# A hybrid decoder layer on one core: another order of the pieces in the gate and up units, and a regrouped last step

## The chip, the cores and the metric

The kernel runs on one core of one Trainium2 chip. The metric is the device time of one execution in microseconds (us), as the median of several runs. Engines: TensorE (matmul, PE in the rows; its weight loads are PEld), VectorE (DVE), ScalarE (ACT), GpSimd (POOL) and SyncE (SP, which issues most of the loads). A row's L73 is line 73 of the kernel.

## The reference

One layer over 256 tokens of width 2048, in float32, with a hidden width of 5632:

```python
h = h + 0.5 * swiglu(rmsnorm(h, ffn1_norm), ffn1_w_gu, ffn1_w_down)
proj = rmsnorm(h, mix_norm) @ w_in
...                     # spatial gating, Mamba-2 scan, output projection, cross attention
h = h + 0.5 * swiglu(rmsnorm(h, ffn2_norm), ffn2_w_gu, ffn2_w_down)
return rmsnorm(h, final_norm)

def swiglu(x, w_gu, w_down):
    g, u = jnp.split(x @ w_gu, 2, axis=-1)
    return (jax.nn.silu(g) * u) @ w_down
```

The change touches the two feed-forward layers (`swiglu`), the making of operands from transposes, and the final norm.

## The kernel before

Every float32 product is made of three float32r products: each operand is split into a high half (a cast on ScalarE, `high`, line 161) and a low half (what is left, a subtraction on VectorE, `split_op`, line 169), and high x high, high x low and low x high are added up. The weights come from memory in pieces of 256 rows by 2 x 512 columns (`load`, on SP's queue, three raw buffers), are split on the way (three buffers for high halves, two for low ones) and are used once.

A feed-forward layer runs in units. A gate and up unit c (0 to 10) computes 512 gate columns and 512 up columns for both token tiles of 128, from eight pieces of the contraction. `proj_sum` takes a piece in one of two ways. A C piece ("ordinary") is 24 matmuls of 512 columns into the four banks m2, m3, m4 and c11, one after another. An S piece forms the product in the manner of Strassen: `split_sums` makes four sums of weight blocks on VectorE, and seven products (21 matmuls) go into the banks m2, m3, m4 and four more, m1, m6, m5 and m7, which only S pieces use. An S piece so spares TensorE three matmuls and costs VectorE more. Its first products (m1, m2, m3) need the plain blocks, the later ones the sums. When the last S piece of a unit has its four own banks done, `mid` adds them up into four parts (line 503; m1 is copied by ScalarE, line 470), and in the last piece of the unit `evac` adds each of the four other banks to a part as it is finished, applies SiLU (ScalarE, line 527) and multiplies gate and up (line 530).

`GU_KINDS = "CSCSCSCC"` gives the kind of each piece of the contraction; `order` the order in which they are taken. Unit c = 0 has kinds and an order of its own (`FIRST_KINDS`, `FIRST`): six C pieces, an S piece, a C piece. All other units take theirs in the order of the string. After units 0 to 4, and after units 5 to 10, `add_sum` multiplies the hidden chunks with the down weights, in two halves with pieces of both kinds (`DN_KINDS`, C C S at the start).

The hidden chunk of a unit (512 columns, two pieces of the next product's operand) is put off by one step with `later`: after the first piece of the following unit, TensorE transposes its two halves into two banks of the same eight that the products use (tag "bank"), four transposes each. A half is then emptied by `to_operand` (for a C piece: high half on ScalarE, line 346, low half on VectorE, line 347) or by `Pieces.sums` (for an S piece: a copy on ScalarE, line 417, then from SBUF three differences and two splits, lines 424 to 430). With a norm's weights as a scale (`c0` given), `to_operand` works on the two columns of its bank by themselves, lines 352 and 353. Nothing else is put off into the units c > 0; jobs that fall between the first and the last S piece wait until it is over.

The matmuls keep their order in the program; the order on the other engines is fixed when the kernel is built, by a planner that goes by readiness and program order, except where `behind` puts an instruction behind another on its engine.

At the end, `finish(n, t, added)` runs for each quarter n of the width and token tile t, behind the last addition to it (`added`): squares on ScalarE with a running sum, the multiplication by the norm's weights, and for n = 3 the reciprocal root (two small VectorE steps, a power on GpSimd) and the scaling of all four quarters with their output transfers (256 KB each, on SP's, ScalarE's or GpSimd's queue). The two scalings of token tile 0 on VectorE are held until the last addition to token tile 1 (`scale_first`).

Of the kernel before, what the change touches and what calls it, by code (L numbers as in the profile page):

```python
# [8 lines left out]
F32 = mybir.dt.float32  # L9
F32R = mybir.dt.float32r  # L10
AF = mybir.ActivationFunctionType
ALU = mybir.AluOpType
AX = mybir.AxisListType
# [3 lines left out]
P = 128  # L17
D = 2048
S = 256
NT = S // P  # L20
DFF = 5632
# [9 lines left out]
EPS = 1e-6  # L31
BIG = 3.0e38
NC = 512
# [13 lines left out]
def hybrid_layer(ctx: ExitStack, tc: tile.TileContext, x, mem, w_gu1, w_dn1, w_in, w_s, w_out,  # L47
                 w_q, w_kv, w_o, w_gu2, w_dn2, cols, rows, gm_vn, fin, out):
    nc = tc.nc
# [11 lines left out]
    small = ctx.enter_context(tc.tile_pool(name="small", bufs=2))  # L61
# [37 lines left out]
    h = [const.tile([P, NT, NC], F32, name=f"h{n}") for n in range(4)]  # L99
# [7 lines left out]
    col = const.tile([P, N_COLS], F32, name="col")  # L107
# [44 lines left out]
    def behind(instructions):  # L152

        order = ExitStack()
        for ins in instructions:
            order.enter_context(tc.issue_after(ins))
        return order
# [87 lines left out]
    def proj_sum(w, r0, xps, kinds, cs, mid, evac, order=None, fine=0):  # L245
        n = len(kinds)
        order = list(range(n)) if order is None else order
        s_at = [m for m, i in enumerate(order) if kinds[i] == "S"]
        c_at = [m for m, i in enumerate(order) if kinds[i] == "C"]
        banks = {}  # L250

        def product(name, pairs, stop):
            start = name not in banks
            if start:
                banks[name] = side("acc")
            seq = [x for ah, al, bh, bl in pairs for x in ((ah, bh), (ah, bl), (al, bh))]
            for m, (a, b) in enumerate(seq):
                matmul(banks[name], a, b, start=start and m == 0, stop=stop and m == len(seq) - 1)

        for m, i in enumerate(order):  # L260
            end = m == n - 1
            key = (id(w), r0, i, cs)
            sums = kinds[i] == "S"
            raw = ready.pop(key) if key in ready else load(w, r0 + i * KP * P, cs, FOR_SUMS if sums else PLAIN)
            if sums:
                parts = split_sums(raw)
                x = xps[i]
                names = ["m1", "m2", "m3", "m6", "m5", "m7", "m4"]
                if m == s_at[-1]:
                    names = ["m1", "m6", "m5", "m7", "m2", "m3", "m4"]  # L270
                for name in names:
                    f, b = {**SOWN, **SHARED}[name]
                    product(name, [(x[:, 0, f], x[:, 1, f], *parts[b])],
                            m == s_at[-1] if name in SHARED else end)
                    if m == s_at[-1] and name == "m7":
                        mid([banks[k] for k in ("m1", "m6", "m5", "m7")])
            else:
                x = xps[i]
                with behind(xps.made[i] if m < fine else ()):
                    hi, lo = split(raw, m < fine)  # L280

                turns = [((t, j), range(KP)) for t, j in HOME]
                if m < fine:
                    turns = [((t, j), (k,)) for k in range(KP) for j in range(2) for t in range(NT)]
                for a, ((t, j), ks) in enumerate(turns):
                    name = HOME[t, j]
                    product(name, [(*tokens(x, k, t), hi[:, 2 * k + j], lo[:, 2 * k + j]) for k in ks],
                            m == (c_at[-1] if name == "c11" else n - 1))
                    if end and ks[-1] == KP - 1:
                        evac(t, j, banks[name])  # L290
                    if a == len(turns) // 2 - 1:
                        step(shut=s_at[0] <= m < s_at[-1], of=0.5)
                step(shut=s_at[0] - 1 < m < s_at[-1], of=0.5)
                continue
            step(shut=s_at[0] - 1 < m < s_at[-1])
# [27 lines left out]

    def sum_sq(ss, src):
        junk = half_k(F32, "junk")
        nc.scalar.activation(junk, src, AF.Square, accum_out=ss)

    def rstd_of(ss, name):
        n = ss.shape[1]
# [8 lines left out]
    def to_operand(srcs, dst, q, c0=None, of=None):  # L338
        of = q if of is None else of
        ps = side("tpose").rearrange("p (k s) -> p k s", k=2)  # L340
        for k in range(2):
            for t in range(NT):
                transpose(out=ps[:, k, t * P:(t + 1) * P],
                          in_=srcs[t][:, (of + k) * P:(of + k + 1) * P], identity=ident)
        if c0 is None:
            hi = nc.scalar.copy(out=dst[:, q:q + 2, :S], in_=ps)
            lo = nc.vector.tensor_tensor(out=dst[:, q:q + 2, S:], in0=ps,  # L347
                                         in1=dst[:, q:q + 2, :S].bitcast(F32), op=ALU.subtract)
        else:
            for k in range(2):  # L350
                sc = col[:, c0 + of + k:c0 + of + k + 1]
                hi = nc.scalar.activation(dst[:, q + k, :S], ps[:, k, :], AF.Copy, scale=sc)
                lo = nc.vector.scalar_tensor_tensor(out=dst[:, q + k, S:], in0=ps[:, k, :], scalar=sc,
                                                    in1=dst[:, q + k, :S].bitcast(F32),
                                                    op0=ALU.mult, op1=ALU.subtract)
        return hi.ins, lo.ins
# [146 lines left out]
        nc.vector.tensor_tensor(out=out, in0=a, in1=b, op=op)  # L503


    GU_KINDS = "CSCSCSCC"

    FIRST_KINDS, FIRST = "CCCCCSCC", [0, 2, 4, 6, 1, 3, 5, 7]

# [2 lines left out]
    def ffn(nrm, w_gu, w_dn, done=None, each=None, fine=0):  # L512
        for c_from, c_to in ((0, 5), (5, 11)):
            kinds, turn = DN_KINDS[c_to - c_from]
            hts = Pieces(kinds, "hid", nrm.xts)
            for c in range(c_from, c_to):
                m = {}
                gs = []

                def mid(banks):  # L520
                    m["m1"], m["y"], m["z"], m["y2"] = parts_of(banks)

                def evac(t, j, ps):
                    g, u = (m["z"], m["y2"]) if t else (m["m1"], m["y"])
                    if j == 0:
                        total(g, ps, g, ALU.subtract if t else ALU.add)
                        nc.scalar.activation(g, g, AF.Silu, scale=nrm.rstd[:, t:t + 1])
                        return
                    total(u, ps, u)
                    nc.vector.scalar_tensor_tensor(out=g, in0=u, scalar=nrm.rstd[:, t:t + 1], in1=g,  # L530
                                                   op0=ALU.mult, op1=ALU.mult)
                    gs.append(g)

                if c == 0:
                    proj_sum(w_gu, 0, nrm.xts, FIRST_KINDS, (c * NC, DFF + c * NC), mid, evac, FIRST, fine)
                else:
                    proj_sum(w_gu, 0, nrm.xts, GU_KINDS, (c * NC, DFF + c * NC), mid, evac)
                hts.later(gs)
            last = c_to == 11
            add_sum(w_dn, c_from * NC, hts, (kinds, kinds), turn, 0.5, done if last else None, each if last else None)  # L540
# [480 lines left out]

    fws = {}

    scale_first = []

    def finish(n, t, added):
        if n not in fws:
            fws[n] = half_k(F32, "fw")
            nc.gpsimd.dma_start(out=fws[n], in_=fin[:, n * NC:(n + 1) * NC].broadcast_to([P, NC]))
        sum_sq(ss_f[:, t, n:n + 1], h[n][:, t, :])  # L1030
        if n < 2 or t == 0:
            nc.vector.tensor_tensor(out=h[n][:, t, :], in0=h[n][:, t, :], in1=fws[n], op=ALU.mult)
        if n < 3:
            return
        if t:

            with behind([added.ins]):
                scale_first.pop()()
        r = rstd_of(ss_f[:, t:t + 1, :], f"f{t}")

        def scale(m):
            o = h[m][:, t, :]
            if m < 2:
                nc.scalar.mul(o, o, r)
            elif t:
                nc.vector.scalar_tensor_tensor(out=o, in0=o, scalar=r, in1=fws[m], op0=ALU.mult, op1=ALU.mult)
            else:
                nc.vector.tensor_scalar(out=o, in0=o, scalar1=r, scalar2=None, op0=ALU.mult)
            queue = nc.sync if m > 1 else nc.scalar if t else nc.gpsimd
            queue.dma_start(out=o_v[:, t, m * NC:(m + 1) * NC], in_=o)  # L1050

        for m in (0, 1):
            if t:
                scale(3 - m)
            scale(m)
        if not t:
            scale_first.append(lambda: (scale(3), scale(2)))

    ffn(n2, w_gu2, w_dn2, each=finish)
    assert not put_off  # L1060
# [31 lines left out]
```

## Time and profile before

| | |
|---|---|
| median of 3 runs | 2500.37 us (2499.86 to 2500.73) |
| the profiled execution | 2500.98 us |
| its span, first to last instruction | 2499.2 us |
| TensorE busy / weight loads busy | 2467.2 us / 2104.5 us |
| VectorE busy | 1967.4 us |
| ScalarE busy | 1291.7 us |
| granted TensorE clock | 0.999 |

The span lies inside the profiled time; the terms of a sum are read from the span's rows and set against that execution's own time. Busy times are shares of the whole span; what a wait costs is read from the stretch in which it stands.

### The profile page before, as it was taken

To read this page: it belongs to the slowest core of one execution; us is meant where nothing else is said; L and a number is where in the kernel's file an instruction comes from. 1 tells how busy PE (TensorE), PEld (TensorE's weight loads), DVE (VectorE), ACT (ScalarE), POOL (GpSimd) and SP (SyncE) were. 2 spreads that over 40 slices of the span, in tenths; PEclk is the share of its full clock that TensorE was granted. 3 is DMA by queue.
4 is the path that set the end of the run, shared out by engine and by line. 5 is a ranking of instruction groups with operands and counts; after the bars stand their busy time and mean duration, and the time that the engine had idled before them with its cause. 6 is when DMAs were issued, how large, how long until landed. Compare 5 with 4: busy or idle time off the path is not lost.

```text
span 2499.2 us, 31437 instructions
## 1 busy us (share of the span) xinstructions
PE 2467.2 (99%) x12673; PEld 2104.5 (84%) x12673; DVE 1967.4 (79%) x1832; ACT 1291.7 (52%) x1164; POOL 20.6 (1%) x46
## 2 busy tenths in 40 slices
PE   9999999999999999999999999999999999999998
PEld 7888887888889998888888999988887888878886
DVE  7988889888877677655698755678899888898887
ACT  6555445555546454435555544455555545455554
POOL 0000000000000000000000000000000000000000
PEclk9999999999999999999999999999999999999999
DMA  7655665565654555545566655555555666656664
GB/s 239 194 195 188 205 207 191 188 196 190 202 178 165 194 182 201 203 152 187 186 199 202 219 170 168 169 180 174 191 195 189 200 198 199 194 185 206 197 203 151
DMA packets 205762, 476.75 MB, mean 191 GB/s; under 512 B 15040, under 2 KB 17248, under 8 KB 204848
## 3 DMA queue, kind: packets, MB, share of 16 engines
q1 hardware_dynamic: 202800, 464.31, 57.0%
q0 software_dynamic: 1840, 9.26, 1.0%
q8 instruction: 99, 1.62, 0.3%
q10 hardware_dynamic: 976, 1.18, 0.1%
q14 instruction: 47, 0.39, 0.0%
HBM read 472.57 MB, written 2.13 MB: 190 GB/s over the span
## 4 chain that ended last, share of the span: by engine, by line
PE 81%; DVE 9%; issue 7%; ACT 2%; DMA 1%; SPq 0%; DVEq 0%; POOL 0%; POOLq 0%; ACTq 0%
PE acc L73 77%; DVE lo L169 3%; ACT hi L161 2%; DVE part L503 2%; DVE sum L169 1%; PE tpose L76 1%; DVE part L530 1%; PE yp L73 1%; PE logits L73 0%; PE o L73 0%; DVE hid L347 0%; DVE cacc L622 0%; DMA raw<-in_w_dn 0%; DMA raw<-in_w_gu 0%; PE mixed L73 0%
## 5 line engine op out<-in xcount | busy, mean ns | idle before, releaser
L161 ACT CAST hi<-raw 128x2048 fp32r<-128x2048 f32 (+1 forms) x438 | 791.3, 1807 | 865.0 <-PE acc L73 726.9
L169 DVE TENSOR_TENSOR lo<-raw,hi 128x2048 fp32r<-128x2048 f32 (+2 forms) x446 | 949.3, 2130 | 327.5 <-PE acc L73 223.3
L73 PE MATMUL acc<-hi,xp_ffn 128*128 128x512 f32 x1824 | 576.0, 390 | 0.4 <-ACT hi L183 0.4
L73 PEld LDWEIGHTS acc<-hi,xp_ffn 128*128 128x128 f32 x1824 | 342.4, 188 | 72.1 <-ACT hi L183 1.1
L73 PE MATMUL acc<-lo,xp_ffn 128*128 128x512 f32 x912 | 355.2, 389 | 0.4 <-DVE lo L169 0.4
L169 DVE TENSOR_TENSOR lo<-sum,hi 128x2048 fp32r<-128x2048 f32 x109 | 249.8, 2292 | 45.3 <-ACT hi L161 45.3
L73 PE MATMUL acc<-hi,hid 128*128 128x512 f32 x896 | 282.6, 390 | 0.0
L161 ACT CAST hi<-sum 128x2048 fp32r<-128x2048 f32 x109 | 208.8, 1915 | 93.2 <-DVE sum L169 75.9
L73 PE MATMUL acc<-hi,xt_mix 128*128 128x512 f32 x768 | 241.7, 393 | 0.0
L73 PEld LDWEIGHTS acc<-lo,xp_ffn 128*128 128x128 f32 x912 | 171.3, 188 | 36.7 <-DVE lo L169 1.4
L73 PEld LDWEIGHTS acc<-hi,hid 128*128 128x128 f32 x896 | 168.2, 188 | 34.7
L73 PE MATMUL acc<-xt_mix,hi 128*128 128x256 f32 x1024 | 186.0, 284 | 0.0
L73 PE MATMUL acc<-lo,hid 128*128 128x512 f32 x448 | 174.5, 390 | 0.0
L503 DVE TENSOR_TENSOR part<-acc,part 128x512 f32<-128x512 f32 x240 | 160.8, 686 | 14.0 <-ACT part L470 7.3
L73 PEld LDWEIGHTS acc<-hi,xt_mix 128*128 128x128 f32 x768 | 144.2, 188 | 30.3 <-issue 0.5
L73 PEld LDWEIGHTS acc<-xt_mix,hi 128*128 128x128 f32 x1024 | 159.6, 192 | 0.3
L73 PE MATMUL acc<-hi,xp_ffn1s 128*128 128x512 f32 x466 | 151.6, 393 | 8.0 <-DVE hid L347 8.0
L73 PE MATMUL acc<-hi,xp_ffn2s 128*128 128x512 f32 x466 | 151.6, 393 | 8.0 <-DVE hid L347 8.0
L169 DVE TENSOR_TENSOR sum<-sum,raw 128x512 f32<-128x512 f32 x218 | 150.4, 690 | 5.2
L73 PE MATMUL acc<-lo,xt_mix 128*128 128x512 f32 x384 | 149.7, 390 | 0.0
L73 PE MATMUL acc<-xt_mix,lo 128*128 128x256 f32 x512 | 145.2, 284 | 0.7 <-DVE lo L169 0.7
L169 DVE TENSOR_TENSOR sum<-raw 128x1024 f32<-128x1024 f32 x109 | 132.7, 1217 | 0.0
(280 smaller groups left out, 3377.8 us busy)
## 6 DMA issues: line engine op xcount, KB each, us to landing
raw<-in_w_gu SPq DMA_DIRECT2D x286, 512.0 KB, 3.9
raw<-in_w_in SPq DMA_DIRECT2D x80, 1024.0 KB, 5.1
raw<-in_w_dn SPq DMA_DIRECT2D x60, 1024.0 KB, 5.4
raw<-in_w_gu SPq DMA_DIRECT2D x132, 256.0 KB, 4.1
raw<-in_w_kv SPq DMA_DIRECT2D x28, 1024.0 KB, 5.3
raw<-in_w_out SPq DMA_DIRECT2D x21, 1024.0 KB, 5.6
raw<-in_w_q SPq DMA_DIRECT2D x16, 1024.0 KB, 5.1
raw<-in_w_dn SPq DMA_DIRECT2D x28, 512.0 KB, 4.0
```

The source lines that it names most:

```text
L73: return pe(nc.tensor.matmul(out, lhsT=lhsT, rhs=rhs, start=start, stop=stop))
L76: return pe(nc.tensor.transpose(out=out, in_=in_, identity=identity))
L161: nc.scalar.copy(out=t[:, :n], in_=x[:, :n])
L169: last_split[:] = [nc.vector.tensor_tensor(**kw).ins]
L503: nc.vector.tensor_tensor(out=out, in0=a, in1=b, op=op)
L530: nc.vector.scalar_tensor_tensor(out=g, in0=u, scalar=nrm.rstd[:, t:t + 1], in1=g, op0=ALU.mult, op1=ALU.mult)
```

## The change

The units c > 0 take their pieces in the order 0, 2, 1, 4, 3, 6, 5, 7, which makes their kinds C C S C S C S C. In `to_operand` with a scale, both high halves are issued before both low halves. In `finish`, the sum over the first three quarters of the squares is made ahead (`pre`), so that one small step is left behind the last squares; all four scalings of token tile 0, on ScalarE too, now stand behind the last addition and the last squares of token tile 1; and each token tile is scaled in the order 3, 0, 2, 1.

```diff
     def sum_sq(ss, src):
         junk = half_k(F32, "junk")
-        nc.scalar.activation(junk, src, AF.Square, accum_out=ss)
+        return nc.scalar.activation(junk, src, AF.Square, accum_out=ss)
...
+            scs = [col[:, c0 + of + k:c0 + of + k + 1] for k in range(2)]
             for k in range(2):
-                sc = col[:, c0 + of + k:c0 + of + k + 1]
-                hi = nc.scalar.activation(dst[:, q + k, :S], ps[:, k, :], AF.Copy, scale=sc)
-                lo = nc.vector.scalar_tensor_tensor(out=dst[:, q + k, S:], in0=ps[:, k, :], scalar=sc,
+                hi = nc.scalar.activation(dst[:, q + k, :S], ps[:, k, :], AF.Copy, scale=scs[k])
+            for k in range(2):
+                lo = nc.vector.scalar_tensor_tensor(out=dst[:, q + k, S:], in0=ps[:, k, :], scalar=scs[k],
...
-    GU_KINDS = "CSCSCSCC"
+    GU_KINDS, GU_ORDER = "CSCSCSCC", [0, 2, 1, 4, 3, 6, 5, 7]
...
-                    proj_sum(w_gu, 0, nrm.xts, GU_KINDS, (c * NC, DFF + c * NC), mid, evac)
+                    proj_sum(w_gu, 0, nrm.xts, GU_KINDS, (c * NC, DFF + c * NC), mid, evac, GU_ORDER)
...
-        sum_sq(ss_f[:, t, n:n + 1], h[n][:, t, :])
+        squares = sum_sq(ss_f[:, t, n:n + 1], h[n][:, t, :])
...
+        if n == 2:
+
+            pre[t] = small.tile([P, 1], F32, name=f"pre{t}", bufs=1)
+            nc.vector.tensor_reduce(out=pre[t], in_=ss_f[:, t:t + 1, :3], axis=AX.X, op=ALU.add)
+            nc.vector.tensor_scalar(out=pre[t], in0=pre[t], scalar1=1.0 / D, scalar2=EPS, op0=ALU.mult, op1=ALU.add)
         if n < 3:
             return
         if t:
 
-            with behind([added.ins]):
+            with behind([added.ins, squares.ins]):
                 scale_first.pop()()
-        r = rstd_of(ss_f[:, t:t + 1, :], f"f{t}")
+        r = small.tile([P, 1], F32, name=f"rstd_f{t}", bufs=1)
+        ms = small.tile([P, 1], F32, name="ms")
+        nc.vector.tensor_scalar(out=ms, in0=ss_f[:, t, 3:4], scalar1=1.0 / D, scalar2=pre[t], op0=ALU.mult, op1=ALU.add)
+        nc.gpsimd.tensor_tensor(out=r, in0=ms, in1=neghalf[:, :1], op=ALU.pow)
...
-        for m in (0, 1):
-            if t:
-                scale(3 - m)
-            scale(m)
-        if not t:
-            scale_first.append(lambda: (scale(3), scale(2)))
+        def scale_all():
+            for m in (3, 0, 2, 1):
+                scale(m)
+
+        if t:
+            scale_all()
+        else:
+            scale_first.append(scale_all)
```

## Rows read from the trace of the kernel before

**Rows 1.** The page's busy times: us, share of the span, instructions.

```profile
PE 2467.2 (99%) x12673; PEld 2104.5 (84%) x12673; DVE 1967.4 (79%) x1832; ACT 1291.7 (52%) x1164; POOL 20.6 (1%) x46
```

**Rows 2.** TensorE's waits, whole span: waiter, awaited, us, times, longest.

```profile
PE acc L73 <- DVE hid L347: 16.1, 16, 1.3
PE acc L73 <- DVE lo L169: 3.4, 9, 0.8
```

**Rows 3.** Busy times of stretches from transpose to transpose: stretch, length, each engine.

```profile
63.95:106.40 42.45, 42.45 (x193) 35.10 (x192) 38.31 (x33) 22.58 (x16) 0.00 (x0) 1.00 0.61 198
106.40:238.36 131.96, 128.00 (x574) 105.29 (x573) 117.54 (x108) 69.00 (x53) 0.00 (x0) 1.00 0.60 195
385.46:602.91 217.45, 213.38 (x956) 175.50 (x955) 192.20 (x168) 113.28 (x83) 0.00 (x0) 1.00 0.61 196
1871.03:2002.99 131.96, 128.00 (x574) 105.32 (x573) 117.63 (x108) 68.90 (x53) 0.00 (x0) 1.00 0.60 195
2150.09:2367.57 217.48, 213.39 (x956) 175.50 (x955) 192.34 (x168) 113.22 (x83) 0.00 (x0) 1.00 0.60 195
```

**Rows 4.** Timeline, unit c = 2: start, us, engine, line, tiles [idle before].

```profile
107.19 0.48 PE L73 MATMUL acc<-hi,xp_ffn1s 128*128 128x512 f32 x1
...
108.09 2.28 DVE L169 TENSOR_TENSOR lo<-raw,hi 128x2048 fp32r<-128x2048 f32 x1
...
111.43 0.68 DVE L347 TENSOR_TENSOR hid<-tpose,hid 128x512 fp32r<-128x512 f32 x1
...
112.17 0.50 PE L73 MATMUL acc<-hi,xp_ffn1s 128*128 128x512 f32 x1 [1.32 <-DVE hid L347]
```

**Rows 5.** Timeline around the end of unit c = 0, and of c = 1.

```profile
52.54 2.28 DVE L169 TENSOR_TENSOR lo<-raw,hi 128x2048 fp32r<-128x2048 f32 x1
...
53.06 0.39 PE L73 MATMUL acc<-hi,xp_ffn 128*128 128x512 f32 x1
...
63.79 2.28 DVE L169 TENSOR_TENSOR lo<-sum,hi 128x2048 fp32r<-128x2048 f32 x1
...
64.74 0.48 PE L73 MATMUL acc<-hi,xp_ffn1s 128*128 128x512 f32 x1
...
85.67 2.28 DVE L169 TENSOR_TENSOR lo<-raw,hi 128x2048 fp32r<-128x2048 f32 x1
```

**Rows 6.** VectorE's groups by shape, 107 to 284 us, those of the hidden chunks.

```profile
L429 DVE TENSOR_TENSOR hids<-forms,hids 128x512 fp32r<-128x512 f32 x6 | 4.1, 684 | 0.0
L347 DVE TENSOR_TENSOR hid<-tpose,hid 128x512 fp32r<-128x512 f32 x5 | 3.3, 685 | 0.5 <-ACT hid L346 0.5
...
L424 DVE TENSOR_TENSOR forms<-forms 128x256 f32<-128x256 f32 x3 | 1.3, 418 | 0.0
```

**Rows 7.** Timeline at the start of the first down projection, which takes C C S.

```profile
241.03 1.29 DVE L347 TENSOR_TENSOR hid<-tpose,hid 128x512 fp32r<-128x512 f32 x2 [0.46 <-ACT hid L346]
243.32 2.29 DVE L169 TENSOR_TENSOR lo<-sum,hi 128x2048 fp32r<-128x2048 f32 x1 [1.00 <-ACT hi L161]
...
244.69 0.39 PE L73 MATMUL acc<-hi,hids 128*128 128x512 f32 x1
```

**Rows 8.** Timeline at the kernel's start.

```profile
7.42 0.47 ACT L352 ACTIVATE xp_ffn<-tpose,col 128x256 fp32r<-128x256 f32 x1 [0.55 <-DVE xp_ffn L353]
...
9.18 0.50 PE L73 MATMUL acc<-lo,xp_ffn 128*128 128x512 f32 x1 [0.22 <-DVE lo L169]
```

**Rows 9.** Timeline of the end; the transfers' rate in 40 slices, 2485 to 2500 us.

```profile
2489.45 0.69 DVE L464 SCALAR_TENSOR_TENSOR h<-acc,h 128x512 f32<-128x512 f32 x1
...
2490.20 1.33 ACT L1044 ACTIVATE h<-h,rstd_f 128x512 f32<-128x512 f32 x2 [0.66 <-POOL rstd_f L334]
...
2491.44 0.61 ACT L326 ACTIVATE junk<-h 128x512 f32<-128x512 f32 x1
...
2492.61 0.58 POOL L334 TENSOR_TENSOR rstd_f<-ms,neghalf 128x1 f32<-128x1 f32 x1 [0.23 <-DVE ms L333]
...
GB/s 0 0 0 0 0 0 0 0 0 0 0 0 0 0 0 0 0 180 371 361 360 366 404 361 350 55 289 388 393 361 388 393 366 230 0 0 0 0 0 0
```

More of the change, by code (lines that the diff above doesn't have):

```diff
@@ L1022, in hybrid_layer @@
     fws = {}
-    scale_first = []
+    scale_first, pre = [], {}
     def finish(n, t, added):
```

## The prediction

> **What bounds the kernel now.** I began with the busy times by engine [rows 1]. TensorE is busy 2467.2 of the 2499.2 us, so 32 us of the span are without a matmul, and a change that issues the same matmuls, as this one does, can only win from those 32 us and from what a stopped TensorE needs to come up to pace again. Next came the list of TensorE's waits [rows 2]: 16 waits of about 1 us, 16.1 us in all, are for line 347, the VectorE half of `to_operand` that empties a transpose bank of a hidden chunk. 3.4 us more are waits for a weight's low half, nine of them; the rest is single waits at the start and the time before the first and after the last matmul.
>
> The third view, the busy times of stretches [rows 3], gives the true price of those waits. I cut it at the transposes that each gate and up unit issues after its first piece, so a stretch is a whole number of units. The stretch without a wait takes 42.45 us and TensorE is busy in all of it: that is the floor of a unit. Three units take 131.96, five take 217.45 and 217.48. So the waits cost 131.96 - 3 x 42.45 = 4.61 and 217.45 - 5 x 42.45 = 5.20 us in the first feed-forward layer, 4.61 and 5.23 in the second, 19.65 us together: 16.1 idle, 3.5 in slower first matmuls behind the stops.
>
> The timeline of one such unit shows the mechanism [rows 4]. The first S piece begins at 107.19, right behind the transposes. It opens its last four banks one after another; of the eight, four are held by the C piece before it and two by the transposes. VectorE does the low half of a C piece first (108.09, 2.28 us) and reaches the hidden chunk's bank at 111.43. The matmul that wants this bank starts at 112.17, after 1.32 us of idleness. What is late is VectorE's turn, not its strength: it is busy 38.31 of the 42.45 us.
>
> **The new piece order.** No matmul, split or load is added or dropped. The units go C C S C S C S C instead of C S C S C S C C. Read across the boundary both are three C pieces and then S C S C S, so loads on SP's queue, raw buffers and splits follow one another as now; only the boundary moves one C piece back. The transposes still come after the unit's first piece, but then a second C piece follows, which opens no bank, and only then the S piece. A C piece lasts (63.95 - 53.06)/2 = 5.45 us, the left edge of the first stretch being where the transposes stand [rows 3, 5]. So VectorE has 5.45 us more before anyone wants the bank, against a wait of 1.32. I take all 19.65 us as won; the bounds are 0 and 19.65.
>
> What this needs is that VectorE isn't late elsewhere, since the four parts and the four evacuations now follow the last S piece with one C piece left in the unit, not two. The trace of before has this boundary once, because the unit c = 0 already ends in S C [rows 5]. With its last C piece beginning at 53.06 and the next S piece at 64.74 (11.68 later), VectorE had done parts, evacuations and the S piece's splits by 63.79 + 2.28 = 66.07, 13.0 after the last S piece; they are first needed after nine matmuls of 5.45/24 = 0.227 us, at 11.68 + 2.04 = 13.7, and no wait stands there. In the new order the S piece begins a C piece later, and its last low half is due at 13.7 + 5.45 = 19.2. VectorE has in addition a C piece's low half (2.29) and the hidden chunk: at most three sums of 0.42 and three low halves of 0.69, 3.3 us [rows 6]. 13.0 + 2.29 + 3.3 = 18.6, which is 0.6 us in time even from that start. An ordinary unit starts better: there the low half of the piece after the last S piece begins at 85.67, 4.4 before that S piece ends (106.40 - 3 x 5.45 = 90.05), while at the boundary of c = 0 it began at 52.54, 0.5 before. So the margin is about 0.6 at the worst boundary and 0.6 + 3.9 = 4.5 us at the others.
>
> The second likeness is the down projection, which already begins C C S with the same transposes after its first piece [rows 7]. There VectorE emptied both banks from 241.03, began the S piece's last low half at 243.32, and the S piece began at 244.69 without a wait, its last low half (done 245.6) 1.1 us ahead of need.
>
> The Trainium skill speaks against the order: "Perfetto Trace Analysis", section Matmul Optimizations, wants all eight PSUM banks in use. With two C pieces in front, four accumulating banks serve alone for 5.45 us longer; by that rule the unit would gain nothing and the time stay near 2500, by the down projection's rows it loses nothing by it.
>
> **High halves together.** In `to_operand` with a scale the second high half waited 0.55 us for VectorE's first low half [rows 8]; now it follows the first high half, and VectorE's work comes after both. During matmuls this is hidden. At the very start TensorE waits for it: the second kind of product began at 9.18 after waiting for a low half. The gain there is between 0 and 0.55 us; some of it comes back as longer waits for low halves later in c = 0, where such waits of up to 0.8 us stand already [rows 2]. I take 0.1.
>
> On the order itself the Trainium skill ("PSUM — Partial Sum Buffer", section on bank collisions) says that two engines may not be in one bank at a time, even reading; the 0.55 us wait agrees, and by it the gain needs both ScalarE passes ahead of VectorE, as in the diff. It leaves the sum as it is.
>
> **The tail.** The last addition ends at 2489.45 + 0.69 = 2490.14. Its squares start at 2491.44, because ScalarE scales token tile 0 first (1.33 us from 2490.20); rstd is there at 2493.19 [rows 9]. In the new order the squares start at 2490.20, 1.24 sooner. On VectorE the two small pre-sums and token tile 0's two scalings stand ahead of the rest, so I take rstd 1.1 sooner. ScalarE then scales four pieces behind the squares, from about 2490.95 to 2493.6, where it ended near 2493.19 + 1.33 = 2494.5. Of the outputs, eight transfers of 256 KB, the rate row shows traffic from about 2491.4 to 2497.6 with one hole near 2494.4; 2.1 MB at about 375 GB/s need 5.6 us, so they can't end before 2497.0. The value is -0.6. If GpSimd issues token tile 0's two output transfers ahead of the second rstd (it waits for ScalarE's scalings until 2492.3 and then issues), rstd comes near 2493.7 and the tail is 0.6 us longer; if the transfers overlap better, 1.1 shorter.
>
> **Sum.** The profiled execution took 2500.98 us, 0.6 above the median of 2500.37; it spans 2499.2, with 1.8 around it. 2500.98 - 19.65 - 0.1 - 0.6 = 2480.6, and the same -20.35 from the median gives 2480.0.
>
> **The rivals.**
> - *New small waits.* VectorE's order is written when the kernel is built; where evacuations are put ahead of a low half that is due, each of the 20 reordered units may lose 0.2 to 0.5 us. 20 x 0.35 = 7: 2487. For it speaks the margin of only 0.6 at the worst boundary; against it that VectorE's work per unit is unchanged and 4 us below the unit's time.
> - *The wait stays.* If VectorE's order puts the hidden chunk behind the low half of the C piece after the S piece, as it does now, that half can begin only when the S piece does, since there are two buffers for low halves; then 2.29 + 3.3 = 5.6 us pass, and the bank is due after 15 matmuls, at 3.4. TensorE waits about as long as today: 2500, the change without effect. Against it: the hidden chunk is ready 5.45 us before that low half can begin.
> - *VectorE becomes the bound of the unit's start.* If one more low half (2.29) goes ahead of the S piece's splits at every boundary and the 3.9 us head start isn't there, the S piece stalls 2.29 - 0.6 = 1.7 us, 20 times, 34 us: 2500.4 - 20.35 + 34 = 2514, slower. It turns into a loss of 0.2% above (19.65 + 5)/20 = 1.2 us at each unit.
>
> **How the numbers follow.** Full gain 0.74 (2478 to 2482), new small waits 0.13 (2482 to 2493), wait stays 0.08, VectorE bound 0.05. The predicted time is that of the first, 2480.0. Below, 19.65 + 0.55 + 1.1 gives 2479.1 and the runs' own scatter 0.5: 2478. Above I reach into the small waits, to 2490, which leaves about 0.16 outside. Within 0.2% (5 us, about what a measurement of this kernel can tell from no change) lies the wait that stays: 0.08. Faster is 0.87, slower 0.05.
>
> **What would show it.** Right: TensorE's waits for line 347 are gone, unit stretches are near 42.45 us in all units, and TensorE's busy time falls by about 3.5 us; the second rstd ends near 2492.1 less the 20 us. Wrong: waits for low halves (line 169) or for the parts (line 503) at the first or second C piece or the first S piece of a unit, or the same 16 waits for line 347 a piece later.

## The result and the profile after

The changed kernel takes 2479.89 us (median of 4 runs, 2479.59 to 2480.06) against 2500.45 us before (4 runs here, one more than in the table ahead of the prediction): a ratio of 0.9918, 95% interval 0.9901 to 0.9935. Faster by 20.6 us, where 2480.0 was forecast.

The page's busy times of the changed kernel, and TensorE's waits over its whole span:

```profile
PE 2461.7 (99%) x12673; PEld 2105.0 (85%) x12673; DVE 1972.4 (80%) x1834; ACT 1287.9 (52%) x1164; POOL 20.5 (1%) x46
```

```profile
PE acc L73 <- DVE lo L169: 3.9, 9, 0.7
PE idle L73 <- DVE idle L564: 1.3, 1, 1.3
PE acc L73 <- ACT hi L183: 0.9, 1, 0.9
PE tpose L76 <- DMA h<-in_x: 0.6, 1, 0.6
```

The 16 waits for line 347 [rows 2] are gone, and TensorE is busy 5.5 us less with the same 12673 matmuls: most of that is a part of the old price that had stood inside the busy time. Matmuls start every 0.23 us and are shown busy for 0.39 [rows 5], so they overlap; at a stop the overlap is lost, and the first matmul behind it takes 0.50 [rows 4]. The busy times of the same stretches, cut at the transposes as in [rows 3]:

```profile
63.30:105.67 42.37, 42.37 (x192) 35.19 (x191) 38.25 (x33) 22.42 (x16) 0.00 (x0) 1.00 0.60 199
105.67:232.79 127.12, 127.12 (x574) 105.56 (x573) 118.78 (x109) 70.69 (x54) 0.00 (x0) 1.00 0.61 198
379.89:591.83 211.94, 211.94 (x957) 175.82 (x956) 193.84 (x169) 114.52 (x84) 0.00 (x0) 1.00 0.61 198
1861.33:1988.44 127.11, 127.11 (x574) 105.56 (x573) 118.77 (x109) 70.68 (x54) 0.00 (x0) 1.00 0.61 199
2135.54:2347.40 211.86, 211.86 (x956) 175.93 (x955) 193.99 (x169) 114.73 (x84) 0.00 (x0) 1.00 0.61 199
```

TensorE is busy without a break in all of them, 42.37 us to a unit. Line by line against [rows 3] that is 131.96 - 127.12 = 4.84, 217.45 - 211.94 = 5.51, 131.96 - 127.11 = 4.85 and 217.48 - 211.86 = 5.62: 20.82 us, and 0.08 in the unit that had no wait before. So the units alone are as much as the whole gain, and the rest of the change sums to about nothing.

VectorE and ScalarE at a unit's start in the changed kernel (timeline; its transposes start at 105.67, right behind its first C piece, and its S piece begins at 112.00):

```profile
105.92 1.91 ACT L161 CAST hi<-raw 128x2048 fp32r<-128x2048 f32 x1 [3.96 <-PE acc L73]
...
109.20 1.92 ACT L161 CAST hi<-sum 128x2048 fp32r<-128x2048 f32 x1
```

```profile
104.93 1.41 DVE L169 TENSOR_TENSOR sum<-sum,raw 128x512 f32<-128x512 f32 x2
106.26 1.75 DVE L169 TENSOR_TENSOR lo<-raw,hi 128x1536 fp32r<-128x1536 f32 x1
...
109.01 0.68 DVE L347 TENSOR_TENSOR hid<-tpose,hid 128x512 fp32r<-128x512 f32 x1
...
111.15 2.29 DVE L169 TENSOR_TENSOR lo<-sum,hi 128x2048 fp32r<-128x2048 f32 x1 [0.66 <-ACT hi L161]
```

The bank that line 347 empties is free at 109.69, 2.3 us before the S piece begins; in [rows 4] it was empty 4.9 us after the S piece had begun. But the S piece's last low half ends at 111.15 + 2.29 = 113.44, only 0.6 us before it is due (112.00 + nine matmuls, 2.04 us). It had to wait for ScalarE, whose cast of the sums began at 109.20 although the sums were there at 106.3: a C piece's cast and the chunk's own high halves stood first. The same half at the boundary of unit c = 0 waited for ScalarE too:

```profile
68.26 2.29 DVE L169 TENSOR_TENSOR lo<-sum,hi 128x2048 fp32r<-128x2048 f32 x1 [1.00 <-ACT hi L161]
```

### The profile page after: what moved, and what is told of

Same layout as the page of the kernel before. It is cut to its first block, busy times and chain, and to the rows that moved or that the text cites. A ratio compares the mean times of both kernels' runs of the same rounds, so it can differ in the third digit from the quotient of the medians.

```text
span 2478.4 us, 31511 instructions
## 1 busy us (share of the span) xinstructions
PE 2461.7 (99%) x12673; PEld 2105.0 (85%) x12673; DVE 1972.4 (80%) x1834; ACT 1287.9 (52%) x1164; POOL 20.5 (1%) x46
## 4 chain that ended last, share of the span: by engine, by line
PE 96%; DVE 2%; ACT 1%; DMA 1%; issue 1%; POOL 0%; POOLq 0%; ACTq 0%; DVEq 0%; SPq 0%
PE acc L73 92%; PE tpose L76 2%; DVE lo L169 1%; PE yp L73 1%; PE logits L73 0%; PE o L73 0%; ACT hi L161 0%; DVE cacc L625 0%; DMA raw<-in_w_gu 0%; PE mixed L73 0%; PE dt L73 0%; DMA col<-in_cols 0%; PE scores L73 0%; DVE sum L169 0%; PE yo L73 0%
```

## The experiments

The theory: the first S piece of a unit waits for a bank that the transposes hold until VectorE gets to it; distance between the two is all that the new order adds. The rival: the gain is made by where a unit's boundary lies, with its parts and evacuations, and the bank is only the place where TensorE happened to stop. A time is the median of the runs, beside runs of the kernel before on the same chip.

**The new order alone.**

```diff
-    GU_KINDS = "CSCSCSCC"
+    GU_KINDS, GU_ORDER = "CSCSCSCC", [0, 2, 1, 4, 3, 6, 5, 7]
...
-  proj_sum(w_gu, 0, nrm.xts, GU_KINDS, (c * NC, DFF + c * NC), mid, evac)
+  proj_sum(w_gu, 0, nrm.xts, GU_KINDS, (c * NC, DFF + c * NC), mid, evac, GU_ORDER)
```

> The kernel before with the new piece order of the gate and up units alone. Theory (the transposes' banks): the 16 waits for line 347 go, every unit stretch comes to 42.4 us, and all of the gain is here: 2500.4 - 21.0 = 2479.4 us, or 1 us less if the regrouped halves cost something in the middle of the kernel. Rival (the regrouped halves and the end carry a part of the gain): 2482 or more.

2479.15 us against 2499.81: ratio 0.9914, interval 0.9897 to 0.9930. The order alone gives all of the gain; whether it is better by the 0.7 us that lie between it and the whole change, these intervals don't tell. The stretches below show one place where the whole change loses 1.13 us and the order alone doesn't.

**The high halves together, alone.**

```diff
+            scs = [col[:, c0 + of + k:c0 + of + k + 1] for k in range(2)]
             for k in range(2):
-                sc = ...; hi = ...; lo = ...
+                hi = nc.scalar.activation(dst[:, q + k, :S], ps[:, k, :], AF.Copy, scale=scs[k])
+            for k in range(2):
+                lo = nc.vector.scalar_tensor_tensor(out=dst[:, q + k, S:], ...)
```

> The kernel before with the high halves issued together, nothing else. Theory: the first unit starts 0.65 us sooner, and 1.4 us are lost later, because ScalarE's order changes in the attention's output projection, where a low half then comes 0.5 us late: 2501.2 us, with a wait of about 0.5 us on a low half near 1755 us. Rival (the loss in the middle belongs to the new piece order or to chance): 2499.8 us and no such wait.

2501.28 us against 2499.81, ratio 1.0004 (0.9995 to 1.0014): not to be told from no change by the time. The trace tells more. From the 16 transposes in the attention's output projection to the transposes of unit c = 1 of the second feed-forward layer, TensorE has the same work in all kernels. It takes 88.73 us in the kernel before (1739.85 to 1828.58) and with the new order alone, and 89.86 us with the halves together, alone or in the whole change: 1.13 us lost. The place (timeline of ScalarE and VectorE with the halves together, then TensorE's line):

```profile
1751.00 1.90 ACT L161 CAST hi<-raw 128x2048 fp32r<-128x2048 f32 x1
1752.81 1.90 ACT L161 CAST hi<-sum 128x2048 fp32r<-128x2048 f32 x1
```

```profile
1754.73 2.29 DVE L169 TENSOR_TENSOR lo<-sum,hi 128x2048 fp32r<-128x2048 f32 x1 [1.32 <-ACT hi L161]
```

```profile
1757.08 0.50 PE L73 MATMUL acc<-lo,ots 128*128 128x512 f32 x1 [0.54 <-DVE lo L169]
```

The same lines of the kernel before (ScalarE):

```profile
1749.51 1.91 ACT L161 CAST hi<-sum 128x2048 fp32r<-128x2048 f32 x1
1751.33 3.28 ACT L161 CAST hi<-raw 128x2048 fp32r<-128x2048 f32 x2
```

There the sums are cast first and the next piece second. Regrouping four small instructions made the planner put the next piece's cast first; VectorE then idles 1.32 us, and TensorE waits 0.54 for the sums' low half. The rest of the 1.13 us is not in a listed wait. At the kernel's start the expected 0.65 us can't be shown: from the first transposes to those of unit c = 1 the kernel before took 58.68 us, the new order alone 58.99, the halves alone 60.18, the whole change 58.45 and the last step alone 57.96. This scatters by 2.2 us, more than the edit could give; a part of it is the first loads (with the halves alone, ScalarE's casts at 18.92 and 25.53 us waited 4.1 and 4.0 us for one).

**The regrouped last step, alone.** The edit is the part of the diff in `sum_sq` and `finish`.

> The kernel before with the regrouped last step alone. Prediction on record: 0.6 us shorter from the last matmul to the end. Theory after the result: the second reciprocal root is ready 1.2 us sooner but the output transfers end no sooner, so the stretch from the last matmul's end to the span's end stays at 9.8 to 10.0 us: 2500.4 us.

2500.45 us against 2499.81, ratio 1.0002 (0.9992 to 1.0011): no change that can be measured. From the last matmul's end to the span's end: 10.2 us here and 9.9 with the whole change, and 9.8 in the kernel before, with the new order alone and with the halves alone. Nothing is won; whether the 0.1 to 0.4 us are a cost of the edit stays open, since the run with earlier transposes below, with the old last step, takes 10.7. The lines of the changed kernel (its last matmul ends at 2468.44, that of the kernel before at 2489.42), and the transfers' rate in 40 slices from 2464 to 2479 us:

```profile
2469.22 0.63 ACT L326 ACTIVATE junk<-h 128x512 f32<-128x512 f32 x1 [0.66 <-DVE h L465]
...
2470.43 0.55 POOL L1050 TENSOR_TENSOR rstd_f<-ms,neghalf 128x1 f32<-128x1 f32 x1 [1.19 <-DVE ms L1049]
2471.02 1.42 DVE L1057 SCALAR_TENSOR_TENSOR h<-h,rstd_f,fw 128x512 f32<-128x512 f32 x2 [0.67 <-POOL rstd_f L1050]
2471.03 0.59 POOL L1061 DMA_DIRECT2D out<-h  x1
```

```profile
GB/s 0 0 0 0 0 0 0 0 0 0 0 0 0 0 0 0 0 98 366 372 404 202 328 361 388 371 344 415 366 366 317 388 388 126 16 0 0 0 0 0
```

The root is ready at 2470.98, 2.54 us after the last matmul; in [rows 9] it was 2493.19 - 2489.42 = 3.77. So 1.23 us are won there. The transfers start about as long after the last matmul as before (2.0 us) and end no sooner: in [rows 9] the rate fell to 55 once; here it falls to 202 early, and the last two slices carry 126 and 16 GB/s. The early fall fits GpSimd's first transfer, which stands behind the root on GpSimd now (2471.03, 2.59 us after the last matmul); the kernel before issued it 1.80 after:

```profile
2491.22 1.15 POOL L1050 DMA_DIRECT2D out<-h  x2 [1.06 <-ACT h L1044]
```

The last scaling on VectorE ends 1.2 us sooner than before (4.0 against 5.2 us after the last matmul). What the scaling wins, the transfers keep.

**The old order with earlier transposes.** Here the chunk's transposes come in the middle of the unit's first piece, and nothing else moves in the program.

```diff
-                hts.later(gs)
+                hts.later(gs, by=1 if c == c_to - 1 else 0.5)
```

> The old piece order, but the transposes of a hidden chunk come half a C piece sooner, in the middle of the unit's first piece (those that fall to a down projection are left where they were). Theory (the banks that the transposes hold are what the first S piece waits for): 2.7 us more for VectorE against waits of at most 1.3, so most of the waits go without any new piece order: 2480.7 us if all go, at most 2490. Rival (the gain comes from where the boundary of a unit lies, with its parts and evacuations, and the bank is only the place where TensorE happens to stop): the waits move elsewhere and the time stays above 2495.

2487.29 us against 2499.81, ratio 0.9948 (0.9933 to 0.9962). TensorE's waits:

```profile
PE acc L73 <- DVE lo L169: 3.5, 10, 0.7
PE tpose L76 <- DVE part L530: 1.4, 2, 0.7
```

Not one wait for line 347 is left, without the new order, and 12.5 us are won: the bank is what TensorE waited for, and half a piece of distance is enough to end those waits. Three things account for the 8 us that are left to the new order. A unit whose chunk needs sums takes about 42.9 us and not 42.37 (42.91 from 104.22 to 147.13), in delays of which most are too short to be listed; ten units are of this kind. In the first unit of a layer the transposes now wait for the chunk itself (line 530). And from the last matmul's end to the span's end it takes 10.7 us and not 9.8, with the same last step, for which no run shows a cause.

**The new order with later transposes.** The other way round: the transposes come behind the second C piece, right in front of the S piece again.

```diff
-                hts.later(gs)
+                hts.later(gs, by=1 if c == c_to - 1 else 2)
```

> The changed kernel, but the transposes of a hidden chunk come one step later, behind the second C piece and so again right in front of the first S piece (those that fall to a down projection are left). The new piece order, the unit's end and the splits stay. Theory (the banks of the transposes): the waits for line 347 come back, about 1 us in most of the 16 units, and the time goes to 2492 to 2500 us. Rival (the new place of the unit's boundary makes the gain by itself): the time stays within 2 us of 2480 and no wait for line 347 appears.

2487.52 us against 2500.30, ratio 0.9947 (0.9932 to 0.9962): between the two. The waits come back, but eight of them and short:

```profile
PE acc L73 <- DVE hid L347: 3.1, 8, 0.4
```

```profile
109.72 2.29 DVE L169 TENSOR_TENSOR lo<-sum,hi 128x2048 fp32r<-128x2048 f32 x1 [1.65 <-ACT hi L161]
...
115.27 0.69 DVE L347 TENSOR_TENSOR hid<-tpose,hid 128x512 fp32r<-128x512 f32 x1
...
116.01 0.50 PE L73 MATMUL acc<-hi,xp_ffn1s 128*128 128x512 f32 x1 [0.39 <-DVE hid L347]
```

With the S piece beginning at 111.97, VectorE empties the bank by 115.27 + 0.69 = 115.96, 3.99 us after; in [rows 4] it took 111.43 + 0.68 - 107.19 = 4.92. The difference of 0.93 us is that of the waits, 1.32 and 0.39. It stands ahead of the bank already, in the low half of the S piece's sums, which the kernel before had here:

```profile
105.88 2.29 DVE L169 TENSOR_TENSOR lo<-sum,hi 128x2048 fp32r<-128x2048 f32 x1 [0.32 <-ACT hi L161]
```

There it ends 0.98 us after the S piece began, with the later transposes 0.04 after. The evacuations of the unit before stand in front of it: the last ends 3.9 us ahead of the S piece in the kernel before (102.54 + 0.75) and 6.9 us ahead with the later transposes (104.33 + 0.74). Whole units show the same difference: 43.05 us for 43.99, and 42.61 for 43.56. So the expectation held in its direction and not in its size. The rival owns a part: with the transposes right in front of the S piece, as before, the new boundary by itself wins 12.8 us, since the second C piece also gives VectorE time to catch up. The two parts can't be added up: distance alone won 12.5 us, the boundary alone 12.8, both together 20.6.

**S pieces one behind another.** The order is C C C S S S C C.

```diff
-    GU_KINDS, GU_ORDER = "CSCSCSCC", [0, 2, 1, 4, 3, 6, 5, 7]
+    GU_KINDS, GU_ORDER = "CSCSCSCC", [0, 2, 4, 1, 3, 5, 6, 7]
```

> The changed kernel with the unit's order C C C S S S C C: the first S piece still has two C pieces and more between it and the transposes, but S pieces follow one another. Theory (alternation is what keeps VectorE and the single buffers of the sums' halves ahead): behind each S piece the next one's sums can be split only when TensorE has left the buffers, 1.92 us of ScalarE and 2.29 of VectorE against 2.04 us of TensorE work: 2.2 us of waiting twice a unit, 20 units, 88 us: near 2568 us, with the waits on low halves (line 169). Rival (VectorE's total work per unit, 38 of 42 us, is all that counts): 2480 to 2485 us.

2654.32 us against 2500.30, ratio 1.0615 (1.0599 to 1.0631). The waits on low halves are 86.9 us in 57 places. That this is close to the 88 expected is luck: two waits of 2.2 us a unit were expected; eight units have three of 1.4 to 1.8 us, and twelve have two of 1.8 and one for a cast on ScalarE (line 161, 9.5 us in all). The theory holds against its rival; the time is 86 us above the expectation. Matmuls of a unit before its stops and around the third (TensorE's timeline), and the busy times of three stretches there (the third figure from the right is the granted clock):

```profile
79.66 0.62 PE L73 MATMUL acc<-hi,xp_ffn1s 128*128 128x512 f32 x2
...
80.34 0.62 PE L73 MATMUL acc<-hi,xp_ffn1s 128*128 128x512 f32 x2
...
88.46 0.64 PE L73 MATMUL acc<-hi,xp_ffn1s 128*128 128x512 f32 x2
90.88 0.79 PE L73 MATMUL acc<-lo,xp_ffn1s 128*128 128x512 f32 x1 [1.78 <-DVE lo L169]
91.47 1.05 PE L73 MATMUL acc<-hi,xp_ffn1s 128*128 128x512 f32 x2
92.32 0.63 PE L73 MATMUL acc<-lo,xp_ffn1s 128*128 128x512 f32 x1
92.75 1.05 PE L73 MATMUL acc<-hi,xp_ffn1s 128*128 128x512 f32 x2
```

```profile
80.00:86.00 6.00, 4.17 (x18) 2.91 (x17) 4.50 (x4) 3.27 (x2) 0.00 (x0) 1.00 0.29 113
86.00:91.50 5.50, 2.34 (x9) 1.29 (x8) 5.04 (x4) 2.49 (x2) 0.00 (x0) 0.88 0.40 132
91.50:97.20 5.70, 5.70 (x15) 4.45 (x14) 3.19 (x4) 0.00 (x1) 0.00 (x0) 0.52 0.69 237
```

In this unit's third stop (89.10 to 90.88) the granted clock falls; it is 0.52 from 91.5 to 97.2, nearly all of it at the lower of its two levels (1.2 of 2.4 GHz). Three matmuls that took 0.68 us before the stops (79.66 to 80.34) take 92.75 - 91.47 = 1.28. From 91.47 to 97.2 that alone is about 2.8 us; for 20 such units it makes an estimate of 56 us, of the 78 by which the run is longer than the changed kernel and these listed waits (86.9 + 9.5) together. The mean granted clock of the whole run is 0.974, where it was 0.999. So a wait here costs once as a wait and again as a slow clock.

**The order, with the halves together only at the start.**

The kernel before gets the new order and, in `to_operand`, both high halves ahead where `together` holds, which is so for the first layer's operands only. From the edit of `to_operand`:

```diff
+        together = c0 is not None and c0 < C_MIX
...
+            if together:
+                his = [high_of(k) for k in range(2)]
             for k in range(2):
...
+                hi = his[k] if together else high_of(k)
```

> The new piece order, with the high halves together only for the operands of the first feed-forward layer, and the last step as before the change. Theory: the gain of the order alone (2479.2) and 0.3 us at the start: 2478.9 us, no wait of 0.5 us on a low half in the output projection of the attention, and 9.8 us from the last matmul's end to the span's end. Rival (the three parts need one another): 2480 us or more.

2479.26 us against 2500.30, ratio 0.9914 (0.9898 to 0.9931). The stretch of 88.73 us is back and the tail is 9.8 us, as expected. It is not faster than the order alone, and waits on low halves stand in the first unit, 2.7 us in all, as with the whole change: the 0.3 us at the start are not shown.

## Why the prediction was right, step by step

- *The new piece order.* Right in mechanism and nearly in size: 19.65 forecast, 20.82 measured in the same stretches. The floor of 42.45 us was 0.08 too high, and 16 units make 1.3 us of that. The run with the last step alone, in the old order, took 42.40 for the same unit, so most of the 0.08 is not the order's; what it is was not tried.
- *The price of a wait.* Taking it from the stretches and not from the list of waits was what made the number. By the 16.1 us of the list the forecast would have been 3.5 us smaller. In the stretches of [rows 3] TensorE's busy time fell by 4.8 us (725.2 to 720.4), where 3.5 were forecast.
- *VectorE in time.* At the boundary of c = 0 the S piece's last low half was to be done 18.6 us after the last S piece at the latest. It ended at 68.26 + 2.29, 18.1 after (the last C piece began near 63.30 - 2 x 5.45 = 52.40), and no wait stands there. The margin of 4.5 us elsewhere was wrong: it is 0.6 in the unit shown above. VectorE's head start is real, but the term left out ScalarE, whose cast of the sums comes behind the chunk's. Nothing hung on it here; another 0.7 us there would have made waits, as in the rival of small waits.
- *What the wait consisted of.* The mechanism in the prediction was the distance between transposes and S piece. The earlier transposes show that distance by itself ends the waits for line 347. The later transposes show a second part that the prediction didn't have: the new boundary by itself cuts a wait of 1.32 us to 0.39, because VectorE has fewer arrears when the S piece begins. The order does both.
- *All eight banks.* The Trainium skill's advice to use all eight ("Perfetto Trace Analysis", Matmul Optimizations) was read in the prediction as speaking against the order, for a time near 2500. The measured 2479.89 us speak against that reading. Four banks alone for a piece longer cost nothing here: the stretches are busy throughout.
- *High halves together.* Forecast as hidden during matmuls and 0.1 us won at the start. It loses 1.13 us in the attention's output projection; the step of the prediction that failed here is "during matmuls this is hidden": the instructions are, but the planner's order around them changed.
- *The tail.* Forecast -0.6 us, measured +0.1 (9.9 us against 9.8), and +0.4 by itself. The root did come 1.23 us sooner (1.1 forecast), and GpSimd did take the root first. What failed is that the transfers would end sooner with it: they didn't.
- *The sum.* That the time comes within 0.1 us of the forecast is luck: the large term was right, and the errors of the small ones cancel. The units gave 1.3 us more, the projection 1.1 less, the tail 0.7 less than forecast. Between the last transposes (20.17 us sooner than before) and the last matmul (20.98) 0.8 more is won, where the kernel before had one wait of 0.5 us on a low half. The start and the long stretch between the layers, which scatter, make up the rest.

## What to carry to other kernels

When a short side job borrows a buffer from the main loop, put a stretch of the loop that needs no new buffer behind it, and price the wait by comparing a loop turn with and without it: the list of waits misses what the stop costs beside the idle time. Where a planner fixes the order on the other engines, an edit to a few hidden instructions can move the large ones beside them; look at their order, not only at the edit's own cost. And before calling an engine ahead, check the other engine that feeds it.

## What the hardware showed that was not expected

Three stops close together in the S S S order brought the granted clock from 1.00 to 0.52 (from 91.5 to 97.2 us), although TensorE was waiting only 1.4 to 1.8 us at a time; the single stops of 1.32 us per unit in the kernel before left it at 1.00 in every stretch of [rows 3]. The Trainium skill ("TensorE: Matmul & The Clock Gate", section "Wait — 56ns, not 53.3ns?") gives 426.7 ns from start to start of matmuls of 512 columns at the lower level; the 1.28 us for three in the rows above agree.
